# The prompt part of the down-projection computed as seven block products in place of eight

## The chip, the cores and the metric

The kernel runs on one core of a Trainium2 chip. The core has a matrix engine (TensorE, called PE in the profile; PEld is its weight loading), a vector engine (VectorE, DVE), an engine for activations and copies (ScalarE, ACT), a general one (GpSimd, POOL) and a queue that issues transfers (SyncE, SP). Sixteen DMA engines move the bytes. The metric is the device time of one launch in microseconds (us), the median of the runs shown; smaller is better.

## The reference

One layer of a streaming encoder runs over 1024 prompt tokens and 64 sample tokens, with 1024 channels. Everything is float32. The change is to the last matrix product and to queues that serve earlier stages, so the layer is shown from its start:

```python
def encoder_layer(x, ...):
    h = rms_norm(x, g_mix_pre)
    proj = h @ w_in                       # then attention, convolution, memory attention
    ...
    x = x + rms_norm(merged @ w_out, g_mix_post)
    h2 = rms_norm(x, g_ffn_pre)
    up = h2 @ w_ffn_up                    # 1024 -> 2 * 2816
    upc = causal_dwconv(up_full, ffn_dw_w)
    fg, fv = jnp.split(upc, 2, axis=-1)
    x = x + rms_norm((jax.nn.gelu(fg) * fv) @ w_ffn_down, g_ffn_post)   # 2816 -> 1024
```

The hidden row `gelu(fg) * fv` (here G) has 2816 channels, which are 22 blocks of 128 (f = 0 to 21).

## The kernel before, in words

**Precision.** A float32 matrix is split into a high and a low part (`split`: ACT casts the high part, DVE subtracts it), and a product is three matmuls: high by high, high by low, low by high.

**Stages, in order of time.** First the memory keys and values (`mkv`), the normalisation of the input rows and their turning (`xT`); then the input projections, woven with stick-breaking attention; the three branch projections, the output projection, the up-projection with its convolution, and the down-projection.

**The start.** For each of nine input tiles x0 to x8 ACT sums squares (`junk_x`, line 272 before), POOL makes the reciprocal root in two tiny instructions (`rstd_x`, lines 197 and 198), DVE scales the tile (line 277), and PE turns it (line 287). PE's queue holds these turns between the matmuls of `mkv`. SP loads the tiles and the weights meanwhile.

**The up-projection** (lines 1463 to 1553 before) goes block by block: for each f seven products of a two-by-two block scheme, each evicted from PSUM by ACT or DVE (line 1483), then `after(f, j)` in the gaps: the convolution (POOL copies edge columns in lines 1508 to 1510, ACT starts and DVE finishes in line 1513), gelu on ACT, and the product `ga * va` on DVE (line 1530). SP stores the result, channels by tokens, to `d_gu` in memory (line 1531). The accumulators live in three rotating slots of one tile `mf`.

**The down-projection** (lines 1557 to 1700 before) reads `w_ffn_down` and `d_gu` back, splits both, and computes nine token tiles by two halves of 512 output columns: 22 blocks by three matmuls (two for the sample tile, whose high and low parts lie side by side), all with 512 moving columns (lines 1596 to 1599). The first three tiles go together while weights arrive (22 blocks), the others tile by tile. Each half is closed by a square sum on ACT (line 1614), a product with the gain on DVE (line 1615), two POOL instructions (lines 1620 and 1621), a scaled sum on DVE (line 1625) and a store.

**What sets the order.** The program is written instruction by instruction, but a scheduler places each instruction on its engine's queue, by the order of the text and by when it reckons the instruction can run; one whose inputs are there from the start may move ahead of earlier text. On the chip each queue runs strictly in order. Semaphores make an instruction wait for its inputs and for the release of its buffers.

Of the kernel before, what the change touches and what calls it, by code (L numbers as in the profile page):

```python
# [17 lines left out]
P = 128  # L18
# [31 lines left out]
def rows_of(t):  # L50
    return P if t < 8 else TS
# [3 lines left out]
def encoder_step(ctx: ExitStack, tc: tile.TileContext, I, O):  # L55
# [37 lines left out]
    d_os = dp.tile([D, T], F32, name="d_os")  # L93
    d_mg = dp.tile([D, T], F32, name="d_mg")
    d_x1 = dp.tile([T, D], F32, name="d_x1")
    d_gu = dp.tile([FF, NO], F32, name="d_gu")

    def split(hi, lo, src):
        ACT.copy(out=hi, in_=src)  # L99
        DVE.tensor_tensor(out=lo, in0=src, in1=hi.bitcast(F32), op=ALU.subtract)  # L100
# [573 lines left out]
    with ExitStack() as st:  # L674
# [296 lines left out]
        class Weave:  # L971
# [115 lines left out]
            def mix(self, steps):  # L1087
                for i, _ in enumerate(steps):
                    if i % (3 * NK) == 0:
                        self.work((1024, 1024))  # L1090
                    self.now += self.STEP
                    while self.left() and self.take():
                        pass
# [12 lines left out]
                self.until(lambda: not self.left())  # L1106

        weave = Weave()

        def attend(p, S):  # L1110
            units = []
# [405 lines left out]
        return acc  # L1517

    accs = {}

    def after(f, j):

        if j == 0:
            accs[f] = conv(f, 0)
        elif j == 1:
            ACT.activation(accs[f], accs[f], AF.Gelu_apprx_tanh)
            accs[f, "v"] = conv(f, 1)
        elif j == 3:
            ga, va = accs.pop(f), accs.pop((f, "v"))
            DVE.tensor_tensor(out=ga, in0=ga, in1=va, op=ALU.mult)  # L1530
            SP.dma_start(out=d_gu[f * P : (f + 1) * P, :], in_=ga)


    for j in range(7):
# [26 lines left out]
    wd = []  # L1561

    def wd_load(f):
        if f < NF and f >= len(wd):
            hi, lo = ((gp if f < 16 else late).tile([P, D], F32R, name=f"wd{f}{e}") for e in "hl")
            raw = gp.tile([P, D], F32, tag="x1", name=f"wdr{f}", bufs=2)
            SP.dma_start(out=raw, in_=I["w_ffn_down"][0][f * P : (f + 1) * P, :])
            split(hi, lo, raw)
            wd.append((hi, lo))

    GC = 768

    def g_load(f0, nf, t0, nt):

        hi, lo = (gp.tile([P, GC], F32R, tag=f"g{e}", name=f"g{f0}_{t0}{e}", bufs=2) for e in "hl")
        n = nt * nf
        raw = gp.tile([P, GC], F32, tag="gr", name=f"g{f0}_{t0}r", bufs=2)[:, :n]
        SP.dma_start(
            out=raw.rearrange("p (f t) -> p f t", f=nf),
            in_=d_gu[f0 * P : (f0 + nf) * P, t0 : t0 + nt].rearrange("(f p) t -> p f t", p=P),  # L1580
        )
        if nt == TS:
            both = hi[:, : 2 * n].rearrange("p (f h t) -> p f h t", f=nf, h=2)
            split(both[:, :, 0, :], both[:, :, 1, :], raw.rearrange("p (f t) -> p f t", f=nf))
            return both.rearrange("p f h t -> p f (h t)"), None
        split(hi[:, :n], lo[:, :n], raw)
        return tuple(x[:, :n].rearrange("p (f t) -> p f t", f=nf) for x in (hi, lo))

    HALF = (slice(0, 512), slice(512, 1024))

    def down(y, f, g, i, c, e):

        gh, gl = g
        wh, wl = wd[f]
        first, last = f == 0, f == NF - 1
        PE.matmul(y, gh[:, i, c], wh[:, HALF[e]], start=first, stop=False)  # L1596
        PE.matmul(y, gh[:, i, c], wl[:, HALF[e]], start=False, stop=last and gl is None)  # L1597
        if gl is not None:
            PE.matmul(y, gl[:, i, c], wh[:, HALF[e]], start=False, stop=last)  # L1599

    x1s = {}

    def load_x1(t):
        x1s[t] = gp.tile([P, D], F32, tag="x1", name=f"x1_{t}", bufs=2)
        SP.dma_start(out=x1s[t][: rows_of(t)], in_=d_x1[t * P : t * P + rows_of(t), :])

    def close_half(t, y, e, o, ms):
        n = rows_of(t)
        c = HALF[e]
        if t == 8:  # L1610
            ACT.copy(out=o[:n, c], in_=y[TS : 2 * TS, :])
            DVE.tensor_tensor(out=o[:n, c], in0=o[:n, c], in1=y[:n, :], op=ALU.add)
            y = o[:, c]
        ACT.activation(junk[:n], y[:n], AF.Square, scale=1.0 / 32.0, accum_out=ms[:n, e : e + 1])
        DVE.tensor_tensor(out=o[:n, c], in0=y[:n], in1=gpo[:n, c], op=ALU.mult)

    def close(t, o, ms):
        n = rows_of(t)
        r = gp.tile([P, 1], F32, tag="rstd", name=f"fr{t}", bufs=4)
        POOL.tensor_scalar(out=r[:n], in0=ms[:n, 1:2], scalar1=ms[:n, 0:1], scalar2=EPS, op0=ALU.add, op1=ALU.add)  # L1620
# [3 lines left out]
        for c in HALF if t == 7 else (slice(0, D),):  # L1624
            DVE.scalar_tensor_tensor(out=o[:n, c], in0=o[:n, c], scalar=r[:n, 0:1], in1=x1[:n, c], op0=ALU.mult, op1=ALU.add)
            SP.dma_start(out=dst[:, c], in_=o[:n, c])

    def y_banks(t):
        return [yp.tile([P, 512], F32, tag="y", name=f"dn{t}_{e}", bufs=8) for e in range(2)]

    def out_tiles(t):
        return (
            late.tile([P, D], F32, tag="fo", name=f"fo{t}", bufs=2),
            gp.tile([P, 2], F32, tag="fms", name=f"fms{t}", bufs=4),
        )


    first = (0, 1, 2)
    wd_load(0)
    gs = {0: g_load(0, 2, 0, 384)}  # L1640
    wd_load(1)
    wd_load(2)
    ys = {t: y_banks(t) for t in first}
    for f in range(NF):
        wd_load(f + 3)
        if f % 2 == 0 and f + 2 < NF:
            gs[f + 2] = g_load(f + 2, 2, 0, 384)
        if f == 12:
            SP.dma_start(out=gpo, in_=I["g_ffn_post"][0].partition_broadcast(P))
        if f < 4:  # L1650
            after(NF - 1, f)
        if f == 5:
            tp = yp.tile([P, 512], F32, tag="y", name="flT", bufs=8)
            for a in range(2):
                PE.transpose(tp[:88, a * P : (a + 1) * P], flast[:, a * 88 : (a + 1) * 88], ident)
            fo = mf[:88, 7, 256 : 256 + 2 * P]
            ACT.copy(out=fo, in_=tp[:88, : 2 * P])
            for a, nm in enumerate(("ffn_state_prompt", "ffn_state_sample")):
                SP.dma_start(out=O[nm][0, 0].rearrange("r (f c) -> (r f) c", c=P), in_=fo[:, a * P : (a + 1) * P])
            right.close()  # L1660
            late = ctx.enter_context(tc.tile_pool(name="late", bufs=1, reuse_waits="tile"))
            gpo = late.tile([P, D], F32, name="gfpost")
            junk = late.tile([P, 512], BF16, name="junk")
        g = gs[f - f % 2]
        for t in first:
            for e in range(2):
                down(ys[t][e], f, g, f % 2, slice(t * P, (t + 1) * P), e)
    rest = (3, 4, 8, 5, 6, 7)
    CHUNK = ((0, 6), (6, 6), (12, 6), (18, 4))
    chunks = [(t, f0, nf) for t in rest for f0, nf in CHUNK]  # L1670
    loaded = {}

    def load_chunk(i):
        if i < len(chunks):
            t, f0, nf = chunks[i]
            t0 = t * P if t < 8 else TP + 2
            loaded[t, f0] = g_load(f0, nf, t0, rows_of(t))

    load_chunk(0)
    for t in first:  # L1680
        load_x1(t)
        o, ms = out_tiles(t)
        for e in range(2):
            close_half(t, ys[t][e], e, o, ms)
        close(t, o, ms)
    i = 0
    for t in rest:
        load_x1(t)
        y = y_banks(t)
        o, ms = out_tiles(t)  # L1690
        for f0, nf in CHUNK:
            i += 1
            load_chunk(i)
            g = loaded.pop((t, f0))
            for e in range(2):
                for f in range(f0, f0 + nf):
                    down(y[e], f, g, f - f0, slice(0, P), e)
                if f0 + nf == NF:
                    close_half(t, y[e], e, o, ms)
        close(t, o, ms)  # L1700


_INS = [
# [38 lines left out]
```

## Time and profile before

| | |
|---|---|
| median of 3 runs | 2443.49 us (2442.7 to 2444.2) |
| the profiled execution | 2443.15 us, its span 2441.3 us |
| mean granted clock of PE | 0.995 |
| PE busy | 2396.0 us (98%), 15167 matmuls |
| DVE, ACT, POOL busy | 1701.3, 1052.7, 108.3 us |
| moved by DMA | 257.76 MB, all issued by SP but 2.4 MB of instructions |

In the rows of the profile a line reads: start in us, duration, engine, line of the kernel, operation, output <- inputs, shapes; in brackets the idle time before it and what ended that. Rows of windows give, for each stretch of time, the busy time of PE, PEld, DVE, ACT and POOL with the count of instructions, the granted clock, the share of the 16 DMA engines and GB/s.

### The profile page before, as it was taken

How to read it: one execution, taken by the hardware profiler on the slowest of the kernel's cores; microseconds unless marked ns; L12 is line 12 of the kernel's file. 1: busy time of each engine (PE TensorE's matmuls, PEld its weight loads, DVE VectorE, ACT ScalarE, POOL GpSimd, SP SyncE). 2: the span in 40 equal slices, each digit the busy share in tenths (PEclk: the TensorE clock that was granted, in tenths of full speed). 3: DMA queues.
4: the chain of work that ended last, by engine and by line, in shares of the span. 5: the costliest groups of instructions: out<-in, count | busy, mean ns of one | idle time of the engine just before them, and what ended most of it. 6: DMA issues, size and time to landing. Idle time of an engine off the chain costs nothing.

```text
span 2441.3 us, 37738 instructions
## 1 busy us (share of the span) xinstructions
PE 2396.0 (98%) x15167; PEld 2275.5 (93%) x15167; DVE 1701.3 (70%) x2100; ACT 1052.7 (43%) x1979; POOL 108.3 (4%) x263
## 2 busy tenths in 40 slices
PE   8999999999999999999999999998999999999998
PEld 7999999999899999999989999977999999988887
DVE  6687878988656888888887435448988888863221
ACT  7324242423566666676674202146433333333111
POOL 2000000000000000000000000011111110100000
PEclk9999999999999999999999999999999999999999
DMA  8222222222455334334344556222222222145331
GB/s 273 86 69 65 92 67 94 66 83 72 145 161 133 82 96 101 89 96 100 94 145 137 174 183 197 73 81 83 72 76 75 71 80 80 63 131 189 106 86 55
DMA packets 287184, 257.76 MB, mean 106 GB/s; under 512 B 63407, under 2 KB 255555, under 8 KB 287009
## 3 DMA queue, kind: packets, MB, share of 16 engines
q1 hardware_dynamic: 287009, 255.34, 34.6%
q8 instruction: 120, 1.97, 0.3%
q14 instruction: 55, 0.45, 0.1%
HBM read 165.47 MB, written 68.19 MB: 96 GB/s over the span
## 4 chain that ended last, share of the span: by engine, by line
PE 51%; issue 2%; DVE 2%; ACT 1%; POOL 1%; DMA 0%; DVEq 0%; POOLq 0%; ACTq 0%
PE ff L1471 6%; PE ff L1472 6%; PE ff L1473 6%; PE dn L1597 4%; PE dn L1596 4%; PE dn L1599 3%; PE sb L158 1%; PE cv L158 1%; PE cv L157 1%; PE sb L157 1%; PE cv L156 1%; PE sb L156 1%; PE mo L156 1%; PE mo L157 1%; PE mo L158 1%
## 5 line engine op out<-in xcount | busy, mean ns | idle before, releaser
L423 DVE SCALAR_TENSOR_TENSOR acc<-u,cw,acc 128x1118 f32<-128x1118 f32 x240 | 331.6, 1382 | 5.6
L99 ACT CAST whi<-wraw 128x1024 fp32r<-128x1024 f32 x112 | 118.2, 1055 | 299.3 <-PE ca L157 62.6
L816 DVE TENSOR_TENSOR_SCAN r<-r 128x128 f32<-128x128 f32 (+7 forms) x128 | 173.3, 1355 | 58.6 <-ACT r L812 58.0
L156 PE MATMUL g<-hh,whi 128*128 128x362 f32 (+1 forms) x576 | 192.4, 334 | 0.0
L157 PE MATMUL g<-hl,whi 128*128 128x362 f32 (+1 forms) x576 | 190.0, 330 | 0.0
L158 PE MATMUL g<-hh,wlo 128*128 128x362 f32 (+1 forms) x576 | 189.9, 330 | 0.0
L100 DVE TENSOR_TENSOR wlo<-wraw,whi 128x1024 fp32r<-128x1024 f32 x112 | 136.5, 1219 | 35.1 <-ACT whi L99 34.9
L1483 DVE TENSOR_TENSOR mf<-mf,ff 128x548 f32<-128x548 f32 (+1 forms) x161 | 110.3, 697 | 55.1 <-PE ff L1473 55.1
L1513 DVE SCALAR_TENSOR_TENSOR mf<-mf,fw 128x1090 f32<-128x1090 f32 x88 | 119.0, 1352 | 16.5 <-ACT mf L1511 15.8
L811 ACT ACTIVATE be<-z 128x128 f32<-128x128 f32 (+2 forms) x192 | 95.8, 499 | 41.1 <-PE z L840 24.6
L156 PEld LDWEIGHTS g<-hh,whi 128*128 128x128 f32 x576 | 109.2, 190 | 0.2
L157 PEld LDWEIGHTS g<-hl,whi 128*128 128x128 f32 x576 | 108.9, 189 | 0.1
L158 PEld LDWEIGHTS g<-hh,wlo 128*128 128x128 f32 x576 | 108.8, 189 | 0.0
L100 DVE TENSOR_TENSOR atl<-aT,ath 128x512 fp32r<-128x512 f32 (+1 forms) x160 | 99.5, 629 | 10.0 <-ACT ath L99 9.1
L99 ACT CAST ath<-aT 128x512 fp32r<-128x512 f32 (+1 forms) x160 | 87.1, 550 | 42.7 <-PE aT L867 26.9
L817 DVE TENSOR_TENSOR be<-be,r 128x127 f32<-128x127 f32 (+7 forms) x128 | 96.2, 754 | 2.7
L812 ACT ACTIVATE r<-z 128x128 f32<-128x128 f32 (+2 forms) x192 | 96.1, 500 | 0.0
L885 PE MATMUL av<-ath,vp 128*128 128x256 f32 x320 | 83.9, 286 | 0.0
L886 PE MATMUL av<-atl,vp 128*128 128x256 f32 x320 | 78.6, 281 | 0.5 <-DVE atl L100 0.5
L547 ACT ACTIVATE gt<-g 128x362 f32<-128x362 f32 (+1 forms) x72 | 33.7, 470 | 92.4 <-PE g L158 90.9
L838 PE MATMUL z<-ks,qd 128*128 128x256 f32 (+2 forms) x192 | 70.6, 369 | 0.0
L99 ACT CAST wf<-wsl 128x512 fp32r<-128x512 f32 x44 | 27.2, 621 | 97.5 <-PE ff L1472 87.5
(1441 smaller groups left out, 7891.1 us busy)
## 6 DMA issues: line engine op xcount, KB each, us to landing
wraw<-in_w_in SPq DMA_DIRECT2D x72, 512.0 KB, 3.9
d_gate<-gt SPq DMA_DIRECT2D x24, 544.0 KB, 3.0
d_gu<-mf SPq DMA_DIRECT2D x22, 545.0 KB, 3.1
vw<-in_w_ffn_up SPq DMA_DIRECT2D x22, 512.0 KB, 3.7
gw<-in_w_ffn_up SPq DMA_DIRECT2D x22, 512.0 KB, 3.7
wdr<-in_w_ffn_down SPq DMA_DIRECT2D x22, 512.0 KB, 4.5
wraw<-in_w_mem_kv SPq DMA_DIRECT2D x16, 512.0 KB, 5.8
qd<-qd SPq DMA_DIRECT2D x24, 272.0 KB, 3.9
```

What stands on the lines that cost most here:

```text
L99: ACT.copy(out=hi, in_=src)
L100: DVE.tensor_tensor(out=lo, in0=src, in1=hi.bitcast(F32), op=ALU.subtract)
L156: PE.matmul(ps, wh[:, k, :], rh[k][c], start=first, stop=False)
L157: PE.matmul(ps, wh[:, k, :], rl[k][c], start=False, stop=False)
L158: PE.matmul(ps, wl[:, k, :], rh[k][c], start=False, stop=last)
L423: DVE.scalar_tensor_tensor(out=acc, in0=u[:, t : t + 1118], scalar=cw[:, t * 8 + i : t * 8 + i + 1], in1=acc, op0=ALU.mult, op1=ALU.add,)
L816: DVE.tensor_tensor_scan(out=rv, data0=rv, data1=rv, initial=1.0, op0=ALU.mult, op1=ALU.min)
L1471: PE.matmul(ps, w[:, k, :], xh[:, k, :], start=k == 0, stop=False)
L1472: PE.matmul(ps, w[:, k, :], xl[:, k, :], start=False, stop=False)
L1473: PE.matmul(ps, w[:, 4 + k, :], xh[:, k, :], start=False, stop=k == 3)
L1483: DVE.tensor_tensor(out=out, in0=a, in1=ps, op=ALU.add)
L1513: DVE.scalar_tensor_tensor(out=acc, in0=raw[:, t : NO + t], scalar=fw[:, t * 44 + m : t * 44 + m + 1], in1=acc, op0=ALU.mult, op1=ALU.add,)
```

## The change

**The product.** With G cut into two channel halves by two token halves and the weight W into two row halves by two column halves (A, C above B, E), the prompt's product is formed from seven products of [512 tokens x 1408 channels] by [1408 x 512 columns], in place of eight. Each runs 4 token tiles x 11 blocks x 3 matmuls of 512 columns, n = 0 to 6 in the table `FORMS`. The results are combined on DVE from PSUM in the tiles `U`, `U3`, `C11`, `C22` (`place`). The sample tile stays plain: its four products ride in n = 0, 1, 4 and 5, which load the plain blocks of the weight.

**Sums of the weight.** Four sums s1 to s4 of quarters of W are made in memory: POOL issues 32 transfers from memory to memory of [352 x 512], 16 that copy (line 1123) and 16 that add into what was copied (line 1125, `accum_op=ALU.add`). In the text one of them is issued every 15 steps of the attention stage.

**Sums of the hidden rows.** `put_down` takes the place of the one store: for f below 11 SP stores x11, x1, t1, t2, t4, t3, xd, with one DVE addition and two ACT negations between; for f from 11 on SP stores x21, x22, x2, and POOL issues five adding transfers (line 1549).

```diff
-    d_gu = dp.tile([FF, NO], F32, name="d_gu")
+    HK = FF // 2
+    d_w = {j: dp.tile([HK, 512], F32, name=f"d_w{j}") for j in ("s1", "s2", "s3", "s4")}
+    d_x = {j: dp.tile([HK, 512], F32, name=f"d_x{j}") for j in ("x11", "x21", "x22", "t1", "t2", "t3", "t4")}
+    d_s = {j: dp.tile([HK, TS], F32, name=f"d_s{j}") for j in ("x1", "x2", "xd")}
...
                 for i, _ in enumerate(steps):
+                    if i % 15 == 7 and down_sums:
+                        down_sums.pop(0)()
...
+        A, B = (w_dn[HK * i : HK * i + HK, 0:512] for i in range(2))
+        C, E = (w_dn[HK * i : HK * i + HK, 512:1024] for i in range(2))
+        down_sums = []
+        for j, first, then in (("s3", A, C), ("s1", C, E), ("s2", A, d_w["s1"]), ("s4", B, d_w["s2"])):
+            rows = [slice(HK // 4 * i, HK // 4 * i + HK // 4) for i in range(4)]
+            down_sums += [lambda j=j, r=r, a=first: POOL.dma_start(out=d_w[j][r, :], in_=a[r, :]) for r in rows]
+            down_sums += [
+                lambda j=j, r=r, a=then: POOL.dma_start(out=d_w[j][r, :], in_=a[r, :], accum_op=ALU.add, max_dma_last_dim=2048)
+                for r in rows
+            ]
...
+    def put_down(f, g, free):
+        r = slice(f % (NF // 2) * P, f % (NF // 2) * P + P)
...
+        if f < NF // 2:
+            put("x11", g[:, LEFT])
+            put("x1", g[:, NEW])
+            DVE.tensor_tensor(out=free[:, LEFT], in0=g[:, LEFT], in1=g[:, RIGHT], op=ALU.add)
+            put("t1", free[:, LEFT])
+            ACT.activation(free[:, RIGHT], free[:, LEFT], AF.Copy, scale=-1.0)
+            put("t2", free[:, RIGHT])
+            put("t4", free[:, RIGHT])
+            ACT.activation(g[:, RIGHT.start : NO], g[:, RIGHT.start : NO], AF.Copy, scale=-1.0)
+            put("t3", g[:, RIGHT])
+            put("xd", g[:, NEW])
+        else:
+            put("x21", g[:, LEFT])
+            put("x22", g[:, RIGHT])
+            put("x2", g[:, NEW])
+            add("t4", g[:, LEFT])
+            add("t2", g[:, RIGHT])
+            add("t3", g[:, RIGHT])
+            add("xd", g[:, NEW])
+            add("t4", g[:, RIGHT])
...
-            SP.dma_start(out=d_gu[f * P : (f + 1) * P, :], in_=ga)
+            put_down(f, ga, va)
...
+    FORMS = (
+        (A, "x11", "x1"), (B, "x21", "x2"), (d_w["s2"], "t2", None), (d_w["s3"], "t3", None),
+        (d_w["s1"], "t1", "x1"), (E, "t4", "xd"), (d_w["s4"], "x22", None),
+    )
...
+    def load_pair(n, k, tiles=None, raw=None):
...
+        for src, hi, lo, t in ((FORMS[n][0], wh, wl, raw[0]), (d_x[FORMS[n][1]], xh, xl, raw[1])):
+            SP.dma_start(out=t[:, :m, :], in_=src[r, :].rearrange("(k p) c -> p k c", p=P))
+            split(hi[:, :m, :], lo[:, :m, :], t[:, :m, :])
...
+    for n in range(6):
+        ys = [y_bank(f"dn{n}_{t}") for t in range(4)]
...
+        for k in range(NF // 2):
...
+            for t in range(4):
+                step(ys[t], n, k, t)
+            if FORMS[n][2]:
+                step_new(new, n, k, n in (0, 4), n in (1, 5))
+            if k % 2 or k == NF // 2 - 1:
+                load_pair(n + 1, k - k % 2)
...
+        for t in range(4):
+            place(n, t, ys[t])
```

**Where the instructions stand.** The scheduler does not leave the 32 transfers of the weight sums in the attention stage: their inputs are there from the start, and they stand at the head of POOL's queue. At the start of the program that queue held before (`rstd_x0` and so on are the reciprocal roots of the input tiles, `ms_x0` the sums that ACT makes):

```order
L82 MEMSET epsc_89 128x1
L197 TENSOR_SCALAR rstd_x0_289<-ms_x0_287 128x1 [waits Activation_49]
L198 TENSOR_TENSOR rstd_x0_289<-rstd_x0_289,mhalf_84 128x1 [waits Pool_49]
L197 TENSOR_SCALAR rstd_x1_296<-ms_x1_294 128x1 [waits Activation_49]
L198 TENSOR_TENSOR rstd_x1_296<-rstd_x1_296,mhalf_84 128x1 [waits Pool_49]
L197 TENSOR_SCALAR rstd_x2_303<-ms_x2_301 128x1 [waits Activation_49]
```

and now, at the same place (`d_ws3` and its like are the sums in memory; DMASW are the semaphores of POOL's transfers; x4 means four such rows):

```order
L82 MEMSET epsc_89 128x1
L1123 DMA d_ws3_105<-in_w_ffn_down 352x512 x4
L1125 DMA d_ws3_105<-in_w_ffn_down 352x512 [waits DMASW0_49]
L1125 DMA d_ws3_105<-in_w_ffn_down 352x512 [waits DMASW1_49]
L1125 DMA d_ws3_105<-in_w_ffn_down 352x512 [waits DMASW2_49]
L1125 DMA d_ws3_105<-in_w_ffn_down 352x512 [waits DMASW3_49]
L1123 DMA d_ws1_103<-in_w_ffn_down 352x512 x2
L201 TENSOR_SCALAR rstd_x0_302<-ms_x0_300 128x1 [waits Activation_49]
L1123 DMA d_ws1_103<-in_w_ffn_down 352x512
L202 TENSOR_TENSOR rstd_x0_302<-rstd_x0_302,mhalf_84 128x1 [waits Pool_49]
L1123 DMA d_ws1_103<-in_w_ffn_down 352x512
L1125 DMA d_ws1_103<-in_w_ffn_down 352x512 [waits DMASW4_49,DMASW0_49]
```

Eleven transfers now stand ahead of the second instruction of `rstd_x0`, 21 ahead of that of `rstd_x3`, and all 32 ahead of those of `rstd_x5` to `rstd_x8`; every adding transfer waits for the copy that it adds to. The rest of that stretch reads, around the tiles x3 and x4:

```order
L201 TENSOR_SCALAR rstd_x3_323<-ms_x3_321 128x1 [waits Activation_49]
L1125 DMA d_ws2_104<-d_ws1_103 352x512 [waits DMASW4_49,DMASW0_49]
L202 TENSOR_TENSOR rstd_x3_323<-rstd_x3_323,mhalf_84 128x1 [waits Pool_49]
L1125 DMA d_ws2_104<-d_ws1_103 352x512 [waits DMASW5_49,DMASW1_49]
...
L1125 DMA d_ws4_106<-d_ws2_104 352x512 [waits DMASW7_49,DMASW3_49]
L201 TENSOR_SCALAR rstd_x5_493<-ms_x5_491 128x1 [waits DVE_49,Activation_49]
```

So the reciprocal roots now stand between transfers that wait for each other. DVE's queue at the start holds the scaling of these tiles between the splits of the memory weights (`wlo`), now:

```order
L104 TENSOR_TENSOR wlo2_237<-wraw2_214,whi2_236 128x1024
L281 TENSOR_SCALAR x0_150<-x0_150,rstd_x0_302 128x1024
L104 TENSOR_TENSOR wlo3_260<-wraw3_240,whi3_259 128x1024
L281 TENSOR_SCALAR x1_228<-x1_228,rstd_x1_309 128x1024
L281 TENSOR_SCALAR x2_254<-x2_254,rstd_x2_316 128x1024
```

Before, the scaling of x0 stood one split earlier; the rest is as it was, and PE's queue is the same up to the turning of x4 (`xT4`) but for single rows. In the up-projection, for f from 11 on, POOL's queue holds between two blocks (`mf` is the tile of the accumulators, DMAHW are semaphores of SP's transfers):

```order
L1529 COPY mf_14638<-mf_14638 128x2
L1549 DMA d_xt4_113<-mf_14638 128x512 [waits DMAHW4_49,DVE_49]
L1549 DMA d_xt2_111<-mf_14638 128x512 [waits DMAHW3_49,Activation_49]
L1549 DMA d_xt3_112<-mf_14638 128x512 [waits DMAHW5_49]
L1549 DMA d_sxd_116<-mf_14638 128x64 [waits DMAHW6_49]
L1549 DMA d_xt4_113<-mf_14638 128x512 [waits DMASW4_49,DMASW0_49]
L1527 COPY mf_14638<-fst_93 128x2 [waits DVE_49,Activation_49,Pool_49]
```

Before, the copies of one block followed those of the block before it with nothing between.

More of the change, by code (lines that the diff above doesn't have):

```diff
@@ L1623, in close @@
         x1 = x1s.pop(t)
[L1624 to L1635, printed above, removed]
@@ L1638, in encoder_step @@
[L1638 to L1667, printed above, removed]
@@ L1668, in encoder_step @@
[L1668 to L1700, printed above, removed]
+        for e, o in halves:
+            DVE.scalar_tensor_tensor(out=o, in0=o, scalar=r[:n, 0:1], in1=x1[:n, HALF[e]], op0=ALU.mult, op1=ALU.add)
+            SP.dma_start(out=dst[:, HALF[e]], in_=o)
```

175 lines of the change are left out of this document (130 added, 45 removed).

## The prediction, made before the changed kernel was run

> **What bounds the kernel now.** I read the page from the top, then windows by stage, then the timelines of the start, of one block of the up-projection and of the end. PE is the bound nearly everywhere:
>
> ```profile
> PE 2396.0 (98%) x15167; PEld 2275.5 (93%) x15167; DVE 1701.3 (70%) x2100; ACT 1052.7 (43%) x1979; POOL 108.3 (4%) x263
> PE   8999999999999999999999999998999999999998
> DMA  8222222222455334334344556222222222145331
> ```
>
> PE is busy in 2396.0 of 2441.3 us. Only the first slice shows the other resource at its limit: the DMA engines are 8 tenths busy there and 2 to 5 later. The windows say it by stage (columns: stretch, length, then busy time and count of PE, PEld, DVE, ACT, POOL; granted clock, DMA share, GB/s):
>
> ```profile
> 0.00:41.00 41.00, 34.93 (x159) 28.02 (x160) 26.05 (x35) 31.65 (x51) 10.57 (x33) 1.00 0.83 287
> 8.00:12.00 4.00, 3.45 (x12) 2.90 (x13) 3.47 (x7) 3.58 (x7) 0.00 (x0) 1.00 1.03 419
> 20.00:30.00 10.00, 10.00 (x53) 8.36 (x52) 6.54 (x8) 8.66 (x14) 3.03 (x7) 1.00 1.00 378
> 1900.00:2000.00 100.00, 100.00 (x789) 100.00 (x789) 84.69 (x109) 39.31 (x52) 12.30 (x30) 1.00 0.22 71
> 2167.00:2172.40 5.40, 0.21 (x3) 0.05 (x1) 5.36 (x6) 4.08 (x5) 0.00 (x0) 0.80 0.19 66
> 2172.40:2179.00 6.60, 6.25 (x17) 4.31 (x18) 5.98 (x6) 2.64 (x3) 0.00 (x0) 0.65 0.66 227
> 2180.00:2260.00 80.00, 80.00 (x355) 66.18 (x354) 32.26 (x29) 27.99 (x30) 0.00 (x0) 1.00 0.60 191
> 2280.00:2430.00 150.00, 150.00 (x663) 124.21 (x662) 31.23 (x38) 22.62 (x43) 5.31 (x10) 1.00 0.24 69
> ```
>
> In the up-projection (1900 to 2000) PE has no gap. The down-projection begins with a gap of 5 us and a slow clock (0.65 in 2172 to 2179), then runs without gaps to its end. At the start the DMA engines are full (1.00 at 378 GB/s, at most 1.03 at 419 in these rows). Whatever takes matmuls out of the down-projection shortens the run; whatever delays PE at the start lengthens it, since nothing later has slack to give it back.
>
> **What the change removes.** Before, the prompt's product takes 8 tiles x 2 halves x 22 x 3 = 1056 matmuls of 512 columns; now 7 x 4 x 11 x 3 = 924. The sample tile has 88 in both (2 x 22 x 2, and 4 x 11 x 2). The pace near the end of the run:
>
> ```profile
> 2424.63 0.39 PE L1596 MATMUL dn<-wd17h,g_896h 128*128 128x512 f32 x1
> 2434.60 0.39 PE L1599 MATMUL dn<-wd21h,g_896l 128*128 128x512 f32 x1
> ```
>
> Between these two starts lie 44 matmuls: 9.97 / 44 = 0.2266 us each. So 132 x 0.2266 = **29.9 us less**.
>
> **What it adds in the down-projection.** Each product loads 11 blocks of two operands of 128 x 512, in 10 pairs of blocks and 2 single ones, each cast on ACT and subtracted on DVE.
>
> ```profile
> L100 DVE TENSOR_TENSOR wlo<-wraw,whi 128x1024 fp32r<-128x1024 f32 x112 | 136.5, 1219 | 35.1 <-ACT whi L99 34.9
> L99 ACT CAST whi<-wraw 128x1024 fp32r<-128x1024 f32 x112 | 118.2, 1055 | 299.3 <-PE ca L157 62.6 <-PE cv L157 62.5 <-PE mo L157 41.8
> L100 DVE TENSOR_TENSOR atl<-aT,ath 128x512 fp32r<-128x512 f32 (+1 forms) x160 | 99.5, 629 | 10.0 <-ACT ath L99 9.1
> L99 ACT CAST ath<-aT 128x512 fp32r<-128x512 f32 (+1 forms) x160 | 87.1, 550 | 42.7 <-PE aT L867 26.9 <-PE aT L873 12.0 <-issue 1.9
> 2433.11 0.69 DVE L1615 TENSOR_TENSOR fo<-dn,gfpost 128x512 f32<-128x512 f32 x1 [10.56 <-ACT junk L1614]
> ```
>
> ACT: 10 x 1.06 + 2 x 0.55 = 11.7 us, DVE: 10 x 1.22 + 2 x 0.63 = 13.5 us, per product of 132 x 0.2266 = 29.9 us. DVE adds at most sixteen operations on 128 x 512 (n = 5: four tiles with two from PSUM or with the gain and two closing ones) at 0.69 us, 11 us. Both fit under PE, as does the traffic: 22 x 0.26 MB = 5.8 MB in 29.9 us is 193 GB/s, what the window 2180 to 2260 shows at a DMA share of 0.60. Operands are loaded one product ahead, so the cover is a whole product. Without that cover each of the six boundaries between products would cost PE about one load and split, what the gap of 5 us at the stage's start shows, 30 us in all; I take 0, since a product's operands are asked for 30 us ahead. The start has the same gap as now. The end has one more DVE operation, 0.7 us, between the last matmul and the last store.
>
> **What it adds in the up-projection.** One block, as it is now:
>
> ```profile
> 1908.83 1.21 ACT L1511 ACTIVATE mf<-mf,fw 128x1090 f32<-128x1090 f32 x1 [0.28 <-DVE mf L1483]
> 1912.09 1.21 ACT L1511 ACTIVATE mf<-mf,fw 128x1090 f32<-128x1090 f32 x1 [0.51 <-DVE mf L1483]
> 1917.10 1.29 DVE L1530 TENSOR_TENSOR mf<-mf 128x1090 f32<-128x1090 f32 x1
> 1903.42 0.49 POOL L1508 COPY mf<-fst 128x2 f32<-128x2 f32 x1 [17.44 <-DVE mf L1483]
> 1903.85 0.18 POOL L1509 COPY mf<-mf 128x2 f32<-128x2 f32 x1
> 1903.97 0.66 POOL L1510 COPY mf<-mf 128x2 f32<-128x2 f32 x1
> 1924.77 0.49 POOL L1508 COPY mf<-fst 128x2 f32<-128x2 f32 x1 [17.44 <-DVE mf L1483]
> ```
>
> A block takes 1924.77 - 1903.42 = 21.35 us. For f below 11 DVE gets one addition of 0.6 us and ACT two negations of about 0.6; DVE is 85% busy and ACT 39% in the window above, so PE covers it: 0. For f from 11 on POOL issues five adding transfers after the product on DVE, which ends at 1918.4. The next block's copies start 6.4 us later, and ACT needs them 1908.83 - 1903.42 = 5.4 us after that: 11.8 us for the five issues and one wait, of the second t4 for the first, less 1.3 for the three copies themselves. The trace shows no transfer issued by POOL. SP's issues of such tiles land in 3.1 us:
>
> ```profile
> d_gu<-mf SPq DMA_DIRECT2D x22, 545.0 KB, 3.1
> ```
>
> At 1 us an issue and 3 to 4 for the wait it fits, and I take 0; at 3 us an issue the convolution is late by about 8 us for ten blocks, of which some 3 are absorbed: 50 us is the upper end.
>
> **What it adds at the start.** This is the largest term. The 32 transfers of the weight sums stand at the head of POOL's queue, ahead of or between the reciprocal roots of the input tiles. Before:
>
> ```profile
> 2.15 0.10 POOL L82 MEMSET epsc<- 128x1 f32 x1
> 13.34 0.22 POOL L197 TENSOR_SCALAR rstd_x<-ms_x 128x1 f32<-128x1 f32 x1 [11.09 <-ACT junk_x L272]
> 23.43 0.57 POOL L198 TENSOR_TENSOR rstd_x<-rstd_x,mhalf 128x1 f32<-128x1 f32 x1
> 40.55 0.57 POOL L198 TENSOR_TENSOR rstd_x<-rstd_x,mhalf 128x1 f32<-128x1 f32 x1
> 41.15 0.75 DVE L277 TENSOR_SCALAR x<-x,rstd_x 128x1024 f32<-128x1024 f32 x1 [0.77 <-POOL rstd_x L198]
> 40.90 0.49 PE L287 MATMUL xT<-ident,x 128*128 128x128 f32 x3
> 41.96 1.64 PE L287 MATMUL xT<-ident,x 128*128 128x128 f32 x13 [0.57 <-DVE x L277]
> ```
>
> POOL is free from 2.2 us, and `rstd_x7` is made at 41.1; DVE scales x7 at once, and PE is already waiting: it idles 0.57 us for DVE before its turn at 41.96. There is no slack. PE's queue has x4 to x7 at that place still, and DVE's splits of the memory weights stand behind the scaling of x0, so PE cannot pass. It stands still for as long as POOL reaches `rstd_x7` later than 41 us.
>
> When does it? All 32 transfers must be issued, and each quarter of s4 is added only when s2 has landed, which waits for s1: by then at least 30 of them have moved, if two are in flight. A transfer has 352 x 512 x 4 = 0.721 MB, and 16 copy, 14 add. In the same time SP's loads up to there have to move: 287 GB/s x 41 us = 11.8 MB. Three prices:
> - Lowest: every transfer counts once, at the highest rate of the rows: (30 x 0.721 + 11.8) / 0.419 = 80 us, from 2.2: 82. PE loses 41.
> - An adding transfer reads two things and writes one, so I count it twice: (44 x 0.721 + 11.8) / 0.378, the rate of the window with a share of 1.00, = 115, from 2.2: 117. PE loses 76.
> - Highest: memory to memory costs twice as much as memory to SBUF on top: (88 x 0.721 + 11.8) / 0.378 = 199, from 2.2: 201. PE loses 160.
>
> I take the middle one, 75 us: it uses the only row with the engines at exactly their limit. After so long a stop PE's clock starts low; in 2172 to 2179 the slow clock costs 6.6 us for 17 matmuls instead of 3.9: 2.7 us.
>
> The Trainium skill ("DMA: Bandwidth & Descriptors", Anatomy of one DMA) fits a transfer from GpSimd with about 2.0 us + bytes / 436 GB/s, measured from HBM to SBUF: 3.65 us for this size, and 30 in series, as an estimate, 110 us. By that the loss is 71 us and the time 2488; no run here shows it, and the sum above doesn't use it.
>
> **Sum**, with a stop of 75 us, on the profiled execution's 2443.15 us (0.34 us under the median, which changes nothing): - 29.9 + 75 + 2.7 + 0.7 = + 48.5, that is 2491.65, so **2492 us**.
>
> **Rivals.**
> - *Slow adding, same place* (the highest price above): the stop is 110 to 160 us, 2527 to 2577. For it: no row shows a transfer from memory to memory, nor how long POOL needs to write out 352 rows. Against it: the rows of SP's loads and stores show no such cost.
> - *The head of POOL's queue costs little*, the case on the faster side. If POOL's transfers did not share the limit of the DMA engines with SP's, they would need (30 x 0.721) / 0.419 = 52 us, POOL would reach `rstd_x7` at 54, PE would lose 13, and the time would be 2443 - 30 + 13 + 3 = 2429. It decides below a stop of 26 us (29.9 - 2.7 - 0.7), that is when POOL reaches `rstd_x7` before 68 us. Against it: 33.4 MB between 2.2 and 68 us is 508 GB/s, above every row. The trace cannot show sharing, since only SP issues now. The Trainium skill ("DMA: Bandwidth & Descriptors", Issuing engines are not separate DMA queues) has all queues run on the same 16 engines and interleave; by that rule this rival falls.
> - *Stop and gain cancel*: between the two, a stop of 22 to 32 us, 2439 to 2449.
> - *The up-projection waits too*: POOL's five adding transfers hold the convolution's copies for f from 11 on, 20 to 50 us on top of my sum: 2512 to 2542. For it: POOL's next copies come 6.4 us after the product. Against it: the 5.4 us behind them, and PE's queue of seven products per block.
> - *The change does not do what it says*: the text spreads the sums over the attention stage, and the order shows that they stand at the start. Had they run there, the stop would be 0 and the time 2443 - 30 + 1 = 2414. I count this with the second rival, since the queue's order is what runs.
>
> **Chances and range.** My forecast (a stop of 41 to 110 us, 2458 to 2527) has 0.56, slow adding 0.22, the up-projection 0.09, cheap head 0.08, cancelling 0.05. About 0.2% (5 us) is what a measurement of this kernel can tell from no change. Faster 0.08, same 0.05, slower 0.87. The range 2450 to 2580 leaves out the faster and the cancelling cases and a few hundredths above; the forecast's own range is 2458 to 2527.
>
> **What would show it.** Right: POOL's `rstd_x7` near 117 us, PE idle for DVE's scaling of x0 to x7 with a sum of 60 to 90 us before 130 us, DMA share near 1 meanwhile; the down-projection's stretch from its first matmul to the end shorter by 29 us, with no gaps between products; the up-projection's length as before (21.35 us a block). Wrong: if `rstd_x7` comes before 68 us the kernel is faster; if PE shows gaps in the up-projection for f from 11 on, waiting for copies behind POOL's transfers, the third term was mis-sized; if the seven products show PE waiting for splits, the cover I counted is not there.

## The result and the profile after

The changed kernel takes 2567.86 us (median of 4 runs, 2567.16 to 2572.45) against 2443.84 us for the kernel before (median of 4 runs, 2442.7 to 2445.55): a ratio of 1.0509, with a 95% interval of 1.0496 to 1.0522. That is 124 us slower. The forecast was 2492 us (+48.5), and one of its rivals, slow adding at the same place, had 2527 to 2577.

The page of the changed kernel, first engine line and the rows of the 40 slices (64 us each) for PE and DMA:

```profile
PE 2378.3 (93%) x15035; PEld 2258.1 (88%) x15035; DVE 1762.4 (69%) x2177; ACT 1101.5 (43%) x2035; POOL 181.7 (7%) x350
PE   2229999999999999999999999999899999998998
DMA  7774222222225553333336446522233336659654
```

PE has 132 matmuls less but only 17.7 us less busy time, since its granted clock is low at the start (0.54 in the first row below): with the sums alone (run 1) the same 15167 matmuls as before take 2407.8 us in place of 2396.0. In the first three slices it does little. Two windows of the same kernel, in the columns of the prediction (the last three are granted clock, DMA share, GB/s), show that the DMA engines are not full in that time either:

```profile
80.00:120.00 40.00, 4.67 (x13) 3.52 (x13) 2.64 (x3) 0.00 (x0) 7.77 (x12) 0.54 0.66 157
2.00:190.00 188.00, 45.43 (x163) 34.54 (x163) 26.75 (x36) 34.72 (x53) 36.54 (x55) 0.65 0.77 189
```

Over the whole stretch it is a share of 0.77 at 189 GB/s, where the forecast had put 1.00 at 378. The waits in the first 230 us of the changed kernel (engine, line, what it waited for; total, times, longest):

```profile
DVE x L281 <- POOL rstd_x L202: 142.8, 8, 45.0
PE mkv L376 <- DVE wlo L104: 114.2, 3, 41.5
POOL d_ws L1125 <- issue: 103.8, 16, 9.9
POOL d_ws L1123 <- issue: 46.5, 11, 9.5
```

PE waits for DVE's splits of the memory weights, DVE waits for POOL's roots, and POOL stands at its own transfers, 103.8 us ahead of the 16 adding ones. POOL's timeline says how (start, duration, line; in brackets the idle time before):

```profile
74.42 1.02 POOL L1125 DMA_DIRECT2D d_ws<-in_w_ffn_down  x1 [6.37 <-issue]
...
82.11 1.00 POOL L1125 DMA_DIRECT2D d_ws<-in_w_ffn_down  x1 [6.37 <-issue]
...
89.23 1.02 POOL L1125 DMA_DIRECT2D d_ws<-in_w_ffn_down  x1 [5.49 <-issue]
97.16 0.94 POOL L1125 DMA_DIRECT2D d_ws<-in_w_ffn_down  x1 [6.91 <-issue]
...
189.24 0.57 POOL L202 TENSOR_TENSOR rstd_x<-rstd_x,mhalf 128x1 f32<-128x1 f32 x1
```

The adds go out one by one, some 7 to 8 us apart. The page gives the time from the issue of one to its landing, in this row for the eight adds of s2 and s4:

```profile
d_ws<-d_ws POOLq DMA_DIRECT2D x8, 704.0 KB, 6.8
```

So the next add goes out about when the one before has landed. The second instruction of `rstd_x7`, at 40.55 us before, runs at 189.24 us: 148.7 us later, where the forecast had 76. From there the delay stays. First and last start of the group of projection matmuls (`g`) and of one group of the up-projection (`ff`), of the kernel before:

```profile
L156 PE MATMUL g<-hh,whi x576: 322/328/507, 106.6 to 722.6; 128*128 128x362 f32 x120, 128*128 128x364 f32 x72
L1471 PE MATMUL ff<-xa0h,wf x88: 285/290/395, 1685.5 to 2146.8; 128*128 128x274 f32 x88
```

and of the changed kernel, with its first and last matmul of the down-projection from PE's timeline:

```profile
L160 PE MATMUL g<-hh,whi x576: 322/328/648, 257.8 to 875.7; 128*128 128x362 f32 x120, 128*128 128x364 f32 x72
L1490 PE MATMUL ff<-xa0h,wf x88: 285/290/397, 1837.2 to 2297.5; 128*128 128x274 f32 x88
```

```profile
2324.51 0.79 PE L1735 MATMUL dn<-wh,xh 128*128 128x512 f32 x1 [6.64 <-ACT xh L103]
2558.17 0.39 PE L1737 MATMUL dn<-wh,xl 128*128 128x512 f32 x1
```

The account of the 124.9 us between the two spans: + 151.2 at the first projection matmul (257.8 - 106.6), + 151.7 at the first of the up-projection, + 152.1 at the first of the down-projection (2324.5 - 2172.4). From first to last matmul the down-projection takes 233.7 us instead of 262.2, 28.5 less. From its last matmul to the end of the span it is 8.0 us instead of 6.7, 1.3 more. Everything that the change was charged with behind the start came out nearly as forecast; the stop at the start is twice as long.

### The profile page after: what moved, and what is told of

Read it like the earlier page. It is cut to its first block, busy times and chain, and to the rows that moved or that the text cites. A ratio compares the mean times of both kernels' runs of the same rounds, so it can differ in the third digit from the quotient of the medians.

```text
span 2566.2 us, 38158 instructions
## 1 busy us (share of the span) xinstructions
PE 2378.3 (93%) x15035; PEld 2258.1 (88%) x15035; DVE 1762.4 (69%) x2177; ACT 1101.5 (43%) x2035; POOL 181.7 (7%) x350
## 4 chain that ended last, share of the span: by engine, by line
PE 45%; issue 3%; DVE 2%; ACT 1%; POOL 1%; DMA 1%; DVEq 0%; POOLq 0%; ACTq 0%
PE ff L1490 5%; PE ff L1491 5%; PE ff L1492 5%; PE dn L1735 3%; PE dn L1737 3%; PE dn L1736 3%; PE cv L162 1%; PE sb L162 1%; PE sb L161 1%; PE cv L161 1%; PE cv L160 1%; PE sb L160 1%; PE mo L160 1%; PE mo L161 1%; PE mo L162 1%
## 5 line engine op out<-in xcount | busy, mean ns | idle before, releaser
L376 PE MATMUL mkv<-wlo,mh 128*128 128x512 f32 x64 | 28.9, 459 | 114.2 <-DVE wlo L104 114.2
L1735 PE MATMUL dn<-wh,xh 128*128 128x512 f32 x308 | 121.0, 393 | 6.7 <-ACT xh L103 6.6
L1737 PE MATMUL dn<-wh,xl 128*128 128x512 f32 x308 | 120.7, 392 | 0.3 <-DVE xl L104 0.3
L1736 PE MATMUL dn<-wl,xh 128*128 128x512 f32 x308 | 120.7, 392 | 0.2 <-DVE wl L104 0.2
L376 PEld LDWEIGHTS mkv<-wlo,mh 128*128 128x128 f32 x64 | 14.4, 225 | 118.9 <-DVE wlo L104 115.5
L281 DVE TENSOR_SCALAR x<-x,rstd_x 128x1024 f32<-128x1024 f32 (+1 forms) x9 | 6.8, 752 | 143.6 <-POOL rstd_x L202 142.8
L104 DVE TENSOR_TENSOR xl<-dr,xh 128x1024 fp32r<-128x1024 f32 (+1 forms) x42 | 47.6, 1134 | 76.4 <-ACT xh L103 76.1
```

Of the source, the lines that this page charges most:

```text
L1735: PE.matmul(y, xh[:, i, c], wh[:, i, :], start=k == 0, stop=False)
L1736: PE.matmul(y, xh[:, i, c], wl[:, i, :], start=False, stop=False)
L1737: PE.matmul(y, xl[:, i, c], wh[:, i, :], start=False, stop=k == NF // 2 - 1)
```

## The experiments

Theory after the result: POOL's roots come late because POOL's transfers form a chain in which an adding transfer goes alone, so a price by bytes at the full rate of the DMA engines is too low. Rivals: part of the loss is elsewhere; the transfers' traffic, and not POOL's queue, holds PE; a fixed wait belongs to every transfer.

### 1. The sums alone at the head, without the rest of the change

```diff
 (the kernel before)
+    HK = FF // 2
+    d_w = {j: dp.tile([HK, 512], F32, name=f"d_w{j}") for j in ("s1", "s2", "s3", "s4")}
...
+                    if i % 15 == 7 and down_sums:
+                        down_sums.pop(0)()
```

with the list `down_sums` as in the change.

> The kernel before, with the 32 transfers of the weight sums at the head of POOL's queue and nothing else of the change (nothing reads the sums; the down-projection is the plain one). Theory A (the stop at the start and the gain in the down-projection add up): first projection matmul at about 258 us, the time 2443 + 151 = 2594. Rival O (part of the 124 us comes from the down-projection or the up-projection of the changed kernel): below 2580.

Measured: 2593.6 us (one run), and in its trace the first projection matmul stands where it stands in the changed kernel:

```profile
L158 PE MATMUL g<-hh,whi x576: 322/328/507, 257.8 to 873.6; 128*128 128x362 f32 x120, 128*128 128x364 f32 x72
```

The transfers alone cost 2593.6 - 2443 = 151 us. The changed kernel is 26 us below that: stop and gain add up, and nothing is lost in the up-projection or the down-projection. Rival O falls.

### 2. The roots taken off POOL

```diff
+        if name.startswith(("rstd_x", "rstd_mem")):
+            DVE.tensor_scalar(out=r[:n], in0=ms[:n], scalar1=EPS, scalar2=None, op0=ALU.add)
+            return r
         POOL.tensor_scalar(out=r[:n], in0=ms[:n], scalar1=EPS, scalar2=None, op0=ALU.add)
```

> The transfers stay at the head of POOL's queue, but the factors of the input and memory tiles are made on DVE by one addition each (the power is left out, so the tiles are scaled by their mean square and not by its reciprocal root). Theory A (PE stands still only because POOL's roots are queued behind the transfers): the first projection matmul comes at 107 to 115 us, the time is 2416 to 2435; what is queued on POOL behind the transfers (the clearing of u at about 200 us) may cost some of that. Rival B (the transfers' traffic on the DMA engines holds SP's loads at the start): the stop stays above 40 us, 2460 or more, with PE or DVE waiting for loads.

Measured: 2514.4 us (one run). The number hits neither theory; the trace says why. The group that turns the memory keys (`mkT`), the last work of the start, and then the waits of the first 230 us:

```profile
L404 PE MATMUL mkT<-ident,mst x16: 270/272/331, 60.4 to 66.1; 128*128 128x128 f32 x16
```

```profile
DVE acc L430 <- ACT acc L427: 92.7, 1, 92.7
ACT acc L427 <- POOL u L589: 92.6, 1, 92.6
...
PE g L160 <- DVE qml L104: 85.8, 1, 85.8
```

With its roots elsewhere, this group starts at 60.4 us, where it starts at 50.8 before and at 202.0 in the changed kernel, although the transfers move at the same time as there. So of the stop of 151 us only some 10 can be traffic on the DMA engines; the rest is POOL's queue. But POOL's next work, the filling of `u`, stands behind the same 32 transfers, and PE meets it 50 us later: 85.8 us of waiting through ACT and DVE. A stop removed at one place came back at the next instruction of the same queue.

### 3. Copies in place of adds

```diff
-                lambda j=j, r=r, a=then: POOL.dma_start(out=d_w[j][r, :], in_=a[r, :], accum_op=ALU.add, max_dma_last_dim=2048)
+                lambda j=j, r=r, a=then: POOL.dma_start(out=d_w[j][r, :], in_=a[r, :])
```

> The 16 adding transfers at the head of POOL's queue are plain copies of the same size (the sums of the weight are left out, so the seven products get wrong operands of the same shape). Theory C (each transfer is one step of a chain, copies about 3.5 us a step and adds 7.4): 16 x 3.9 = 62 us less than the changed kernel, about 2506. Rival D (a fixed cost of each transfer from POOL, adding or not): no change, about 2568. Rival E (the forecast's price by bytes at 378 GB/s with 32 copies counted once, 94 us until the last root, a stop of 53): 2443 - 27 + 53 + 3 = 2472.

Measured: 2491.3 us (one run). The first and the last of the 32 transfers on POOL, and the first projection matmul:

```profile
2.21 1.47 POOL L1123 DMA_DIRECT2D d_ws<-in_w_ffn_down  x2
...
106.69 0.55 POOL L1125 DMA_DIRECT2D d_ws<-d_ws  x1 [4.02 <-DMA d_ws<-in_w_ffn_down]
```

```profile
L160 PE MATMUL g<-hh,whi x576: 322/328/652, 178.9 to 797.0; 128*128 128x362 f32 x120, 128*128 128x364 f32 x72
```

32 copies take (106.69 - 2.21) / 31 = 3.4 us each, and the stop is 178.9 - 106.6 = 72 us. Adding therefore costs (151 - 72) / 16 = 4.9 us more than copying, per transfer. Theory C was 15 us too high but is the nearest; no change (D) and the price by bytes (E, 2472) are both out. Even without a single add the stop is as long as the forecast had it with all of them. The window of this run up to the last root, and the queues in it (q0 are POOL's transfers, q1 SP's; packets, MB, share of the 16 engines):

```profile
2.00:110.00 108.00, 45.15 (x160) 34.00 (x160) 25.81 (x35) 34.44 (x53) 29.26 (x53) 0.73 0.93 313
q0 software_dynamic: 4821, 22.21, 61.0%
q1 hardware_dynamic: 3538, 11.55, 32.2%
```

With copies alone the engines are nearly full (0.93), but they move 313 GB/s, not the 378 of the forecast: 66 of the 108 us go to POOL's copies, 35 to SP's loads, some 7 are empty. So the copies are not what leaves the engines empty in the changed kernel; the adds, which go alone, are.

What one transfer costs the engines is read from the queues of the changed kernel, first in the 29.1 us of the four adds to s1 (74.4 to 103.5), then in the 12.8 us of the four copies to s4 (150.6 to 163.4):

```profile
q0 software_dynamic: 1472, 2.88, 63.2%
q1 hardware_dynamic: 122, 0.42, 3.6%
```

```profile
q0 software_dynamic: 768, 2.88, 68.1%
```

An add of 0.721 MB uses all engines for 0.632 x 29.1 / 4 = 4.6 us in a step of 7.3, a copy for 0.681 x 12.8 / 4 = 2.2 us in a step of 3.2. SP's traffic (q1) is next to nothing, so the engines stand empty for the rest. The Trainium skill ("Collectives: The Full Stack", The bandwidth ceiling: the fold count and why AG ≠ RS ≠ AR) says of the adding step of a ReduceScatter, a transfer between cores, that each chunk is read from two sources and that this halves its rate against a copy; 4.6 against 2.2 us here has the same ratio, but no run shows that two reads are its cause.

### 4. Wider rows for half of the adds

```diff
+            wide = {"s2": 2, "s4": 4}.get(j, 1)
+            def big(x, n=wide):
+                return x.rearrange("(a b) c -> a (b c)", b=n) if n > 1 else x
...
-POOL.dma_start(out=d_w[j][r, :], in_=a[r, :], accum_op=ALU.add, max_dma_last_dim=2048)
+POOL.dma_start(out=big(d_w[j][r, :]), in_=big(a[r, :]), accum_op=ALU.add, max_dma_last_dim=2048)
```

> The four adding transfers of s2 go in rows of 4 KB (176 x 1024) and those of s4 in rows of 8 KB (88 x 2048); s1 and s3 keep rows of 2 KB and serve as the control. Theory F (an adding transfer's pace is set by its packets of 2 KB, 178 ns each, 22 on each of 16 engines): s2's step falls from about 7.2 us to 5, s4's to 4 or less, and the time by 15 to 25 us, to 2543 to 2553. Rival G (the pace is set by the bytes that the adding unit handles, or by a wait between transfers): all steps stay near 7.2 us and the time near 2568.

Measured: 2559.2 us (one run). The queue of POOL's transfers during the four adds of s2 (124.2 to 154) in this run:

```profile
q0 software_dynamic: 1472, 2.88, 59.1%
```

1472 packets for 2.88 MB, as in the adds with rows of 2 KB above (four copies take 768). The experiment did not change what it was to change: the setting `max_dma_last_dim=2048`, which the edit keeps, cuts the rows to 2 KB again, and in the program built from this kernel all 16 adding transfers of the sums stand as 352 x 512, as they did without the edit. So the run says nothing on wider rows, the steps stayed at 7 us and more, and neither F nor G is tested. What the trace of the changed kernel does show is the time of single packets (medians): 178 ns for 2 KB of an add, 159 ns for 4 KB of a copy, 84 ns for 2 KB of SP's transfers.

The 9 us that this run is shorter come from the order, which the scheduler made anew. The second instruction of `rstd_x4` stood behind 31 of the 32 transfers and stands behind 27 here, that of `rstd_x7` behind 32 and here behind 31; the first projection matmul comes at 248.9 us in place of 257.8.

### 5. The sums pinned to their place in the text

```diff
-                        down_sums.pop(0)()
+                        tc.keep_in_program_order(down_sums.pop(0)())
```

> The 32 transfers of the weight sums are pinned behind what stands before them in the text, so that they run in the attention stage, behind the reciprocal roots of all nine input tiles. Theory A (the whole loss is POOL's late roots at the start, 151 us by the first projection matmul, and the down-projection gains 27 us): the first projection matmul is back at about 107 us and the time is 2443 - 27 = 2416, between 2410 and 2424. Rival B (the transfers cost as much wherever they run, by slowing SP's loads or holding POOL's later work): above 2440, with PE waiting for POOL or for DMA in the attention stage.

Measured: 2445.85 us (10 runs); ratio to before 1.0009, interval 0.9999 to 1.0018. The start is as before again (first projection matmul at 107.6 us), and yet the 27 us are gone: rival B, though not at the price of the head. The transfers now run from 711 to 940 us, in the attention stage. The same stretch of time before, and in this run:

```profile
760.00:840.00 80.00, 77.36 (x525) 73.41 (x526) 62.58 (x93) 53.43 (x134) 0.00 (x0) 1.00 0.44 109
```

```profile
760.00:840.00 80.00, 62.41 (x388) 58.05 (x386) 44.21 (x63) 40.63 (x101) 8.10 (x10) 0.89 0.90 195
```

PE loses 15 us of busy time in these 80, and its granted clock falls to 0.89. In all, the first matmul of the merged output (`mo`) comes 34.4 us later than before (1281.8 against 1247.4), where the first projection matmul came 1.0 later. The DMA engines go from 0.44 to 0.90, and SP's own transfers land later; medians of issue to landing of one kind, before (720 to 930) and here (720 to 960):

```profile
ks<-kh SPq DMA_DIRECT2D x13, 96.0 KB, 2.1
```

```profile
ks<-kh SPq DMA_DIRECT2D x12, 96.0 KB, 6.4
```

Two of the waits that are new between 700 and 960 us, and the largest for POOL, which is 4.3 us before too:

```profile
ACT vs L745 <- DMA out_sb_v_prompt<-vs: 10.1, 1, 10.1
ACT kh L103 <- DMA ks<-kh: 8.4, 1, 8.4
DVE ls L243 <- POOL lnr L242: 4.3, 2, 3.8
```

So there is a second cost beside the queue: traffic, where attention sends keys and queries through memory and waits for them. POOL's queue is not the cause here.

### 6. The sums where POOL is idle and the DMA engines have room

```diff
             POOL.tensor_copy(out=u[:, 1054:1084], in_=cst[:, i * 30 : (i + 1) * 30])
+            for _ in range(min(len(down_sums), (0, 5, 5, 5, 5, 4, 4, 4)[i])):
+                tc.keep_in_program_order(down_sums.pop(0)())
```

and no transfers in `Weave.mix`.

> The same 32 transfers, pinned in groups of 5, 5, 5, 5, 4, 4, 4 behind the filling of u1 to u7 on POOL (about 66 to 520 us), where POOL is idle and the DMA engines were 0.20 to 0.30 busy before. Theory J (the transfers cost PE nothing where POOL has no due work behind them and the DMA engines have room; the losses were POOL's late roots at the head, and traffic in the attention stage at 711 to 950 us): first projection matmul at 107 us, PE without gaps until 650, the time 2443 - 27 = 2416, between 2411 and 2422. Rival K (a transfer from POOL slows the kernel wherever it runs, by DVE's or ACT's accesses or SP's traffic): 2430 to 2446, as in the run before.

Measured: 2418.13 us (4 runs, 2415.72 to 2421.05); ratio to before 0.9898, interval 0.9883 to 0.9912. A window of it with five of the transfers issued in it, and one group on POOL:

```profile
200.00:250.00 50.00, 50.00 (x312) 48.97 (x311) 34.46 (x44) 20.75 (x36) 4.41 (x7) 1.00 0.62 150
```

```profile
346.30 0.98 POOL L590 DMA_DIRECT2D d_ws<-d_ws  x1 [0.28 <-issue]
354.89 0.96 POOL L590 DMA_DIRECT2D d_ws<-d_ws  x1 [7.60 <-issue]
361.67 0.95 POOL L590 DMA_DIRECT2D d_ws<-d_ws  x1 [5.82 <-issue]
368.77 0.94 POOL L590 DMA_DIRECT2D d_ws<-d_ws  x1 [6.15 <-issue]
```

PE has no gap, with the DMA engines at 0.62 (0.24 before in the same window). The same chain at the same pace, 7 to 9 us an add, costs nothing here. Theory J holds: the change is worth 25 us once its transfers lie where nobody waits for POOL and the engines have room. This version is faster than both kernels.

### 7. Halved transfers

```diff
-            rows = [slice(HK // 4 * i, HK // 4 * i + HK // 4) for i in range(4)]
+            rows = [slice(HK // 8 * i, HK // 8 * i + HK // 8) for i in range(8)]
```

on top of 6, with 10 or 8 transfers behind each u.

> As the run with groups behind u, with each transfer cut in two (176 x 512, 64 transfers, 10 or 8 behind each u). Theory L (only one adding transfer of 352 rows is under way at a time, because POOL's store of descriptors holds one and not two; it holds two of 176 rows): two half adds land in less than one whole, 5 to 6 us a pair against about 7.5, since the gap of 2.7 us between whole adds is covered. Rival M (a fixed wait after each adding transfer, whatever its size): a pair of halves takes 9 to 10 us. The time of the kernel is the same in both, about 2416, if theory J holds.

Measured: 2416.4 us (4 runs); ratio to before 0.9892, interval 0.9875 to 0.9908. The same four quarters of s2, now eight transfers:

```profile
346.73 1.77 POOL L590 DMA_DIRECT2D d_ws<-d_ws  x2 [0.22 <-issue]
354.15 0.87 POOL L590 DMA_DIRECT2D d_ws<-d_ws  x1 [5.64 <-issue]
355.99 0.86 POOL L590 DMA_DIRECT2D d_ws<-d_ws  x1 [0.97 <-issue]
359.59 0.87 POOL L590 DMA_DIRECT2D d_ws<-d_ws  x1 [2.74 <-issue]
362.77 0.86 POOL L590 DMA_DIRECT2D d_ws<-d_ws  x1 [2.31 <-issue]
```

Two halves go out together and the third waits, where of the wholes only one goes out. After the first wait a half goes out every (362.77 - 354.15) / 3 = 2.9 us, a pair in 5.8, against (368.77 - 354.89) / 2 = 6.9 for a whole. A fixed wait after each transfer (M) would have made it longer; it falls. Of the 2.7 us in which the engines stand empty in a step, the second half under way covers about 1.

### 8. Longer copies

```diff
+            halves = [slice(HK // 2 * i, HK // 2 * i + HK // 2) for i in range(2)]
-            down_sums += [lambda j=j, r=r, a=first: POOL.dma_start(out=d_w[j][r, :], in_=a[r, :]) for r in rows]
+            down_sums += [lambda j=j, r=r, a=first: POOL.dma_start(out=d_w[j][r, :], in_=a[r, :]) for r in halves]
```

on top of 6, with 4 or 3 transfers behind each u.

> As the run with groups behind u, but the copies that start each sum go as two of 704 x 512 in place of four of 352 x 512 (the adding transfers stay at 352 x 512). Theory L (what limits POOL is how many rows it can hold under way, an adding row counting twice: one add of 352 rows, two of 176, two copies of 352, so only one copy of 704): the second of two copies that stand side by side is issued only when the first has landed, 7 us or more after it, where two copies of 352 rows went out together. Rival N (only adding transfers wait for one another): the two copies of 704 rows go out together. The time of the kernel is that of the run with groups behind u, 2412 to 2422, in both.

Measured: 2417.05 us (4 runs); ratio to before 0.9882, interval 0.9866 to 0.9899. The two copies that begin s3, of 352 rows in run 6 and of 704 rows here:

```profile
67.13 1.48 POOL L588 DMA_DIRECT2D d_ws<-in_w_ffn_down  x2
```

```profile
66.41 0.95 POOL L589 DMA_DIRECT2D d_ws<-in_w_ffn_down  x1
75.11 0.71 POOL L589 DMA_DIRECT2D d_ws<-in_w_ffn_down  x1 [7.75 <-issue]
```

Two plain copies of 704 rows go one by one as well, so it is not the adding that makes a transfer go alone; N falls. Nor is it the number of transfers: in run 7 five copies of 176 rows went out in one go:

```profile
67.59 3.04 POOL L588 DMA_DIRECT2D d_ws<-in_w_ffn_down  x5
```

Two copies of 352 rows under way, one of 704; two adds of 176 rows, one of 352. What fits that is a limit on the rows that POOL has written out and that have not yet landed. It lies at 704 rows of a copy or above, since two of 352 go together, and below 1056, since a third waits. One add of 352 rows stays within it and three of 176 do not, so a row of an add counts as 1.3 to 3 rows of a copy; two would fit. The kernel reserves little room for them (`dynamic_dma_scratch_size=1024`, line 1822); that this sets the limit is argued and not shown, since no run has another size.

## Why the prediction was right or wrong

**The step that failed** is the price of the transfers at the start: "I take the middle one, 75 us: it uses the only row with the engines at exactly their limit." The stop was 151 us, and the engines were busy for 0.77 of the time and not at their limit, where the prediction's own sign of being right was a share near 1. The rows that it went by were those of SP's transfers, which filled the engines. POOL's queue has two copies of this size under way or one add, and the next one goes out when one has landed. The price was that of a stream, and the adds were a chain. In numbers, from 2.2 to 189.2 us, the time until `rstd_x7` (q0 are POOL's transfers, q1 SP's):

```profile
q0 software_dynamic: 8709, 22.59, 56.5%
q1 hardware_dynamic: 4670, 12.86, 20.2%
```

Of these 187 us POOL's transfers took 106, SP's 38, and for 44 the engines stood empty. The forecast's 115 us were 84, 31 and 0. So 44 of the 72 us that it lacks are the gaps of the chain, a term that its sum does not have; 22 are POOL's transfers, each dearer than at 378 GB/s and all 32 in place of 30; 7 are SP's. The condition "if two are in flight" was the place where the gaps could have entered.

**Counting an add twice** was right in kind: 4.6 against 2.2 us of the engines' time, a factor of 2.1. At 378 GB/s the forecast made it 3.8 and 1.9; the steps were 7.3 and 3.2 to 3.4. The Trainium skill's fit ("DMA: Bandwidth & Descriptors", Anatomy of one DMA), quoted in the prediction, gives 3.65 us for one transfer of this size. The 3.4 us between copies of run 3 lie near that, but two copies were under way at a time there, so it is not the same quantity; an add took 6.8 us from issue to landing.

**The upper range was met for another reason.** The rival "slow adding" has 2527 to 2577 and the time is 2568, but its price took every transfer as twice as dear as at 378 GB/s, and a copy from memory to memory runs at 0.721 MB / 2.2 us = 328 GB/s of the engines' time. That the time lies in its range, and so in the outer range of 2450 to 2580, is partly luck: the empty engines, which it did not price, filled it.

**The place of the loss** was right: POOL's roots behind the transfers, DVE's scaling behind the roots, PE behind DVE's splits, no slack to give it back. DVE waited 142.8 us for the roots. After the stop another 151.2 - 148.7 = 2.5 us went, where 2.7 was forecast for the clock; the granted clock in the 12.8 us from `rstd_x7` to the first `mkT` was 0.73, and 1.00 in the same 10.3 us before.

**The cheap head** and **cancelling** fall: `rstd_x7` came at 189 us, not before 68.

**The down-projection** came out as forecast: 28.5 us less between first and last matmul (29.9), the tail 1.3 us longer (0.7), no boundary between products that PE waited at, only the gap at the start, 6.6 us where it was 5.2.

**The up-projection** too: 460.3 us from first to last start of its group, 461.3 before. An issue by POOL takes about 0.9 us there, three of them 2.67, where the forecast took 1:

```profile
2133.47 2.67 POOL L1549 DMA_DIRECT2D d_xt<-mf  x3 [11.40 <-DVE mf L1581]
```

**"Had they run there, the stop would be 0 and the time 2414"**, said of the attention stage, was wrong by 32 us: run 5 has 2445.9. The prediction went only by POOL's queue there and not by the DMA share, 0.44 in that stretch, nor at the transfers that attention waits for. The number is right for a stretch with room (run 6: 2418).

## What to carry to other kernels

Before pricing a transfer by its bytes, ask how many of its kind are under way at once: if the queue lets one go when the last has landed, the price is steps times latency, and a DMA share well below 1 with the issuer waiting at its own issues is the sign of it (0.77 here). Where the share is near 1, as with copies alone (0.93), bytes do price it, but at the rate of that kind of transfer (313 GB/s, not 378). A transfer whose inputs are there from the start may be placed at the head of a queue by the scheduler whatever the text says, so read the order, and pin it behind the work that others wait for. Then choose the place by two rows: the issuer idle, and the DMA share low; this change went from 5% slower to 1% faster by that alone.

## What the runs showed of the hardware that was not expected

- An adding transfer from POOL, memory to memory, with rows of 2 KB moved in packets of 2 KB (1472 for 2.88 MB), a plain copy of the same rows in packets of 4 KB (768). A packet of either kind took about as long (178 and 159 ns), so the add occupied the 16 engines 2.1 times as long (4.6 and 2.2 us for 0.721 MB). Whether wider rows would make it cheaper is open.
- POOL held back the next transfer by rows: five copies of 176 rows, two copies of 352 or two adds of 176 went out together; one copy of 704 or one add of 352 went alone, and the next left 7 to 9 us later.
- With the DMA engines at 0.90 instead of 0.44, SP's transfers of 96 KB took 6.4 us to land instead of 2.1, and PE lost 15 of 80 us of busy time, though the engines were not full.
